# Twelve pairs of the down projection in the 7-product form, with two of the weight sums on GpSimd

## The chip, the core and the metric

The kernel runs on one NeuronCore of a Trainium2 chip. The metric is the device time of one execution in microseconds (us). Five engines work side by side, each through its own instructions in order: TensorE (PE, matmuls; PEld are its weight loads), VectorE (DVE), ScalarE (ACT), GpSimd (POOL) and SyncE (SP, which here only issues loads and stores). An instruction waits for semaphores that other engines raise, and what stands behind it on its engine waits as well.

## The reference

One decoder layer for 256 tokens of width 2048, all in float32: three mixers side by side (pooling, latent attention, attention to a memory), an output projection, and a gated feed-forward part with a short convolution. The change lies in the last part:

```
def conv_glu_ffn(h, w_gate, w_up, conv_w, conv_b, w_down):
    g = h @ w_gate                       # 256 x 5632
    gp = jnp.pad(g, ((0, 0), (CONV_WIDTH - 1, 0), (0, 0)))
    gc = conv_b
    for j in range(CONV_WIDTH):
        gc = gc + conv_w[j] * gp[:, j:j + S]
    return (jax.nn.silu(gc) * (h @ w_up)) @ w_down   # 5632 -> 2048
...
x = x + conv_glu_ffn(rms_norm(x, g_ffn[l]), ...)
```

## The kernel before

**Precision.** Each float32 operand of a large matrix product is split into a rounded high part and a low part, the rest. ACT writes the high part (`wh`, L98), DVE the low part (`wl = raw - wh`, L99), and PE adds three products: high by high, low by high, high by low. A tile of 1024 columns of weights so costs one ACT and one DVE instruction; there are four buffers for `wh` and four for `wl`, and three for raw weights (`wr`), which SP fills with 1 MB loads.

**Gate and up.** The 5632 features are 44 blocks of 128. For each block f, `gemm_pair` computes gate and up (L134), and `glu` adds the halves of the two sums: `halves` copies one half from PSUM on ACT (L784) and adds the other on DVE (L785). For gate this is in the buffer `g`, for up in the buffer `u`, one buffer each. DVE and ACT then make the convolution and the Silu in `gc`, DVE multiplies (L801 or L809), and the result is split as the left operand of the down projection (L158, L159).

**The down projection** takes two blocks at a time, as 22 pairs j, and goes through them twice, once for each half c of the 2048 output columns. A pair is a 2x2 block product: two token halves, two feature blocks, two column quarters of 512.
- A *plain* pair makes 8 block products of 3 matmuls each, 24 matmuls of 128x512, from two weight tiles of 1024 columns.
- A pair in the *7-product form* makes 7 block products, 21 matmuls (the Strassen-Winograd scheme). `glu` prepares its left operand: four sums of 128x128 (L813) and a split of 128x896 (L816, L817), in 7 KB per partition instead of the 4 KB of a plain pair. `seven` makes sums of the weights: `F13` (T1 and T3, one DVE instruction, L880), then T2 = r2 - T1 (L882) and T4 = r3 - T2 (L883), `F24` together. It then splits four tiles: `b11` (512 columns), `b2`, `t13`, `t24` (1024 each).
- `SEVEN` lists the pairs in this form, 11 of 22.

Four PSUM banks hold the sums of one half's own products, four the common products. `common` adds the latter to the residual near the end of a half (L905, L909), `finish` adds the former and stores (L916, L917). The residual comes back from HBM by four GpSimd loads per half (L901). The first half's stores are issued by GpSimd too, in pair 0 of the second half.

**Order.** A scheduler orders each engine's instructions; those marked with `keep` stay in program order. In the down projection all ACT and DVE splits after pair 1 of the first half are kept. The weight tile of every fourth pair goes to a part of `dn` (L850) instead of `wr`. Buffers of `F13` and `F24` are the first four 512-column pieces of `dn`, and swap from one 7-product pair to the next.

**The ring.** GpSimd's own DMAs (`nc.gpsimd.dma_start`) take their descriptors from a ring, whose size per partition is an argument at L1017.

Of the kernel before, what the change touches and what calls it, by code (L numbers as in the profile page):

```python
# [15 lines left out]
ALU = mybir.AluOpType  # L16
# [22 lines left out]
NN = 512  # L39

PAIRS = KF // 2
SEVEN = (1, 2, 4, 5, 7, 9, 11, 13, 15, 17, 19)

VEC = [
    ("g_mix", KD), ("g_ffn", KD), ("g_q_lat", QR // P), ("g_kv_lat", KVR // P),
# [15 lines left out]
def layer(ctx, tc, xT_d, xn_d, memT_d, vec_d, tab_d, w_z_d, w_mqkr_d, w_q_d, w_kv_d, w_mem_d, w_pool_d, w_o_d,  # L61
          w_g_d, w_u_d, w_dn_d, out_d):
    nc = tc.nc
# [8 lines left out]
    def nm(s):  # L72
        uid[0] += 1
        return f"{s}_{uid[0]}"
# [13 lines left out]
    def keep(ins, on=True):  # L88

        return tc.keep_in_program_order(ins) if on else ins  # L90

    def split_w(raw, o, n, cut=HS, kept=False, shift=0):

        hi = stage.tile([P, HS], F32R, tag="wh", name=nm("wh"), bufs=4)
        lo = stage.tile([P, HS + 64], F32R, tag="wl", name=nm("wl"), bufs=4)[:, shift:shift + HS]
        for c in range(0, n, cut):
            e = min(n, c + cut)
            keep(nc.scalar.copy(hi[:, c:e], raw[:, o + c:o + e]), kept)  # L98
            keep(nc.vector.tensor_tensor(lo[:, c:e], raw[:, o + c:o + e], hi[:, c:e].bitcast(F32), op=ALU.subtract),  # L99
                 kept)  # L100
        return hi, lo
# [53 lines left out]
    def split_act(dst, src, scale=None, kept=False):  # L155

        if scale is None:
            nc.scalar.copy(dst[:, 0:T], src)  # L158
            nc.vector.tensor_tensor(dst[:, T:2 * T], src, dst[:, 0:T].bitcast(F32), op=ALU.subtract)  # L159
        else:  # L160
            keep(nc.scalar.activation(dst[:, 0:T], src, AF.Copy, scale=scale), kept)
            keep(nc.vector.scalar_tensor_tensor(dst[:, T:2 * T], src, scale, dst[:, 0:T].bitcast(F32),
                                                op0=ALU.mult, op1=ALU.subtract), kept)
# [4 lines left out]
    def v(name, i=0):  # L168
        o = VOFF[name] + i
        return vec[:, o:o + 1]  # L170
# [610 lines left out]
    def halves(ps, tag):  # L781

        t = fp.tile([P, T], F32, tag=tag, name=nm(tag), bufs=1)
        nc.scalar.copy(t[:], ps[:, 0:T])  # L784
        nc.vector.tensor_tensor(t[:], t[:], ps[:, T:2 * T], op=ALU.add)  # L785
        return t

    def glu(f, psg, psu):
        g = halves(psg, "g")
        nc.vector.tensor_tensor(g[:], g[:], r1[:], op=ALU.mult)  # L790
        gc = fp.tile([P, T], F32, tag="gc", name=nm("gc"), bufs=1)
        nc.scalar.activation(gc[:], g[:], AF.Identity, bias=v("conv_b", f), scale=v("cw2", f))  # L792
        for d, w in ((1, "cw1"), (2, "cw0")):
            nc.vector.scalar_tensor_tensor(gc[:, d:T], g[:, 0:T - d], v(w, f), gc[:, d:T], op0=ALU.mult, op1=ALU.add)  # L794
        nc.scalar.activation(gc[:], gc[:], AF.Silu)
        u = halves(psu, "u")
        j, e = f // 2, f % 2
        if j not in SEVEN:
            if e == 0:
                aT[j] = fp.tile([P, 2, 2 * T], F32R, name=nm("aT"))  # L800
            nc.vector.tensor_tensor(u[:], u[:], gc[:], op=ALU.mult)  # L801
            split_act(aT[j][:, e, :], u[:])
            return
        if e == 0:
            aT[j] = fp.tile([P, 2, 7, P], F32R, name=nm("aS"))
            hold[j] = fp.tile([P, 8, P], F32, tag="s8", name=nm("s8"), bufs=1)
        s = hold[j]
        o = 0 if e else 6
        nc.vector.tensor_tensor(s[:, o:o + 2, :].rearrange("p a t -> p (a t)"), u[:], gc[:], op=ALU.mult)  # L809
        if e:  # L810
            for d, a, op, b in ((2, 7, ALU.add, 1), (3, 2, ALU.subtract, 6), (4, 6, ALU.subtract, 7),
                                (5, 0, ALU.subtract, 3)):
                nc.vector.tensor_tensor(s[:, d, :], s[:, a, :], s[:, b, :], op=op)  # L813
            hi, lo = (aT[j][:, i].rearrange("p a t -> p (a t)") for i in range(2))
            sf = s[:, 0:7, :].rearrange("p a t -> p (a t)")
            nc.scalar.copy(hi, sf)  # L816
            nc.vector.tensor_tensor(lo, sf, hi.bitcast(F32), op=ALU.subtract)  # L817
# [10 lines left out]
    for ps, raw in zip(pss, raws):  # L828
        gemm_t(ps, raw, HS, lambda k: h2[:, k, :], range(8, KD), first=False)
    glu(0, *pss)  # L830
    for f in range(1, KF):
        pss = [ps_main() for _ in range(2)]
        gemm_pair(pss, [load_w(w[f], STG) for w in (w_g_d, w_u_d)], lambda k: h2[:, k, :])
        glu(f, *pss)
# [9 lines left out]
    def load_dn(c, j):  # L844

        cnt[1] += 1
        if cnt[1] % 4:
            return load_w(w_dn_d[c, j], STG)
        raw = dn[:, 4:8].rearrange("p b n -> p (b n)")
        nc.sync.dma_start(raw, w_dn_d[c, j])  # L850
        return raw

    def prod(ps, a, b, first, last):

        nc.tensor.matmul(ps, a[0], b[0], start=first, stop=False)  # L855
        nc.tensor.matmul(ps, a[1], b[0], start=False, stop=False)  # L856
        nc.tensor.matmul(ps, a[0], b[1], start=False, stop=last)  # L857
# [15 lines left out]
    def seven(c, j, own, com, first, last, kept):  # L873
        raw = load_dn(c, j)
        r3 = raw.rearrange("p (b n) -> p b n", n=NN)

        i = cnt[0] % 2
        cnt[0] += 1
        F13, F24 = dn[:, 2 * i:2 * i + 2], dn[:, 2 - 2 * i:4 - 2 * i]
        keep(nc.vector.tensor_tensor(F13, r3[:, 1:3], r3[:, 0:2], op=ALU.subtract), kept)  # L880
        b11 = split_w(raw, 0, NN, kept=kept)
        keep(nc.vector.tensor_tensor(F24[:, 0], r3[:, 2], F13[:, 0], op=ALU.subtract), kept)  # L882
        keep(nc.vector.tensor_tensor(F24[:, 1], r3[:, 3], F24[:, 0], op=ALU.subtract), kept)  # L883
        b2 = split_w(raw, 2 * NN, HS, kept=kept)
        t13 = split_w(F13.rearrange("p b n -> p (b n)"), 0, HS, kept=kept)
        t24 = split_w(F24.rearrange("p b n -> p (b n)"), 0, HS, kept=kept)
        for (b, s), f, ps, own_ in (((b11, 0), 6, com[0], False), ((b2, 0), 5, own[0, 1], True),
                                    ((b2, 1), 0, own[0, 0], True), ((t13, 0), 2, com[1], False),
                                    ((t13, 1), 4, com[3], False), ((t24, 0), 3, com[2], False),
                                    ((t24, 1), 1, own[1, 0], True)):  # L890
            prod(ps, [aT[j][:, i, f, :] for i in range(2)], [w[:, s * NN:(s + 1) * NN] for w in b],
                 first and not own_, last and not own_)
# [29 lines left out]
    for c in range(2):  # L922
        own_ps, com_ps = (ps_main, ps_aux) if c else (ps_aux, ps_main)
        own = {(t, n): own_ps()[:] for t in range(NT) for n in range(2)}
        com = None
        for j in range(PAIRS):
            kept = c > 0 or j > SEVEN[0]
            if j in SEVEN:
                if com is None:
                    com = [com_ps()[:] for _ in range(4)]  # L930
                seven(c, j, own, com, j == SEVEN[0], j == SEVEN[-1], kept)
            else:
                between = None
                if j == 0 and done is not None:
                    between = lambda o=done: finish(0, o, nc.gpsimd)
                elif j >= PAIRS - 2:
                    between = lambda s=j - PAIRS + 3: common(c, com, s)
                plain(c, j, own, j == 0, j == PAIRS - 1, kept, between, j == PAIRS - 1)
            if j == PAIRS - 6:
                common(c, None, 0)  # L940
        done = own
# [85 lines left out]
```

## Time and profile before

| what | value |
|---|---|
| time, median of 3 runs | 1004.43 us (1003.9 to 1004.48) |
| profiled execution: time, span | 1004.47 us, 1002.7 us |
| PE busy | 996.4 us (99%) |
| DVE busy | 767.4 us (77%) |
| ACT busy | 586.6 us (58%) |
| POOL busy | 18.5 us (2%), 39 instructions |
| DMA | 200.17 MB, mean 200 GB/s |

The profile shows one execution. In a *timeline*, a row gives start, duration, engine, line, operation, output<-input, shape and count, and in brackets how long the engine was idle before and what ended that. In a *group* row, the figures behind the bars are busy time and mean ns of one, then idle time before it and what ended most of it. In the view of *busy time by stretch*, each row gives the stretch, its length, then busy time (and count) of PE, PEld, DVE, ACT and POOL, the granted clock of PE, the DMA share and GB/s. Matmuls are pipelined: a row's duration is longer than the distance to the next start.

### The profile page before, as it was taken

The page shows a single profiled execution, that of the slowest core. Times are in us where ns is not written, and L with a number is a line of the kernel's source. Part 1 is how long each engine was busy: PE and PEld are TensorE (multiplying, and loading weights), DVE is VectorE, ACT ScalarE, POOL GpSimd, SP SyncE. Part 2 cuts the span into 40 slices and gives each one's busy share as a digit, 9 for nine tenths or more (in the row PEclk, how much of TensorE's full clock was granted, in tenths as well). Part 3 has the DMA queues.
Part 4 walks back from the last instruction along what each step waited for, and adds up shares of the span by engine and source line. Part 5 has one row for each costly group of instructions (what it writes and reads, how often), then busy time and mean ns, then how long its engine had stood idle before and what let it go on. Part 6 is the DMA issues. An engine that isn't in the chain of part 4 may idle for free.

```text
span 1002.7 us, 14022 instructions
## 1 busy us (share of the span) xinstructions
PE 996.4 (99%) x5342; PEld 859.7 (86%) x5342; DVE 767.4 (77%) x1160; ACT 586.6 (58%) x859; POOL 18.5 (2%) x39
## 2 busy tenths in 40 slices
PE   9999999999999999999999999999999999999998
PEld 8898888888888888888888888888888888888886
DVE  6778689855677776777776767777677998899887
ACT  7678666544566555555555655555565656545562
POOL 1010000000000000000000000000000000010000
PEclk9999999999999999999999999999999999999999
DMA  9867443433664555455555555555556665486651
GB/s 356 294 239 277 151 173 150 157 139 128 229 230 169 186 196 206 171 207 182 197 197 189 203 175 203 190 189 205 190 194 221 221 230 210 169 293 213 220 197 42
DMA packets 31764, 200.17 MB, mean 200 GB/s; under 512 B 3664, under 2 KB 4176, under 8 KB 9808
## 3 DMA queue, kind: packets, MB, share of 16 engines
q1 hardware_dynamic: 28512, 189.04, 52.6%
q0 software_dynamic: 2752, 9.44, 2.7%
q8 instruction: 42, 0.69, 0.3%
q10 hardware_dynamic: 432, 0.79, 0.2%
q14 instruction: 26, 0.21, 0.1%
HBM read 195.06 MB, written 4.19 MB: 199 GB/s over the span
## 4 chain that ended last, share of the span: by engine, by line
PE 96%; DVE 3%; issue 1%; ACT 0%; DVEq 0%; ACTq 0%
PE psm L134 47%; PE psm L117 7%; PE psm L151 5%; PE psm L152 5%; PE psm L153 5%; PE psa L855 3%; PE psa L857 3%; PE psm L857 3%; PE psa L856 3%; PE psm L856 3%; PE psm L855 3%; DVE wl L99 1%; PE psa L679 1%; PE psa L151 1%; PE psa L153 1%
## 5 line engine op out<-in xcount | busy, mean ns | idle before, releaser
L99 DVE TENSOR_TENSOR wl<-wr,wh 128x1024 fp32r<-128x1024 f32 (+2 forms) x338 | 391.4, 1172 | 131.6 <-ACT wh L98 75.2
L98 ACT CAST wh<-wr 128x1024 fp32r<-128x1024 f32 (+2 forms) x338 | 340.4, 1012 | 133.4 <-PE psm L134 55.4
L134 PE MATMUL psm<-h,wh 128*128 128x512 f32 x1376 | 320.1, 390 | 0.0
L134 PEld LDWEIGHTS psm<-h,wh 128*128 128x128 f32 x1376 | 255.1, 188 | 51.3
L134 PEld LDWEIGHTS psm<-h,wl 128*128 128x128 f32 x1376 | 163.8, 188 | 3.3
L134 PE MATMUL psm<-h,wl 128*128 128x256 f32 x1376 | 164.5, 277 | 0.0
L98 ACT CAST wh<-dn 128x1024 fp32r<-128x1024 f32 (+1 forms) x66 | 65.4, 995 | 79.5 <-PE psa L856 31.9
L99 DVE TENSOR_TENSOR wl<-dn,wh 128x1024 fp32r<-128x1024 f32 (+1 forms) x66 | 74.0, 1146 | 16.0 <-ACT wh L98 16.0
L792 ACT ACTIVATE gc<-g,vec 128x256 f32<-128x256 f32 x44 | 26.5, 602 | 93.3 <-DVE g L790 93.3
L794 DVE SCALAR_TENSOR_TENSOR gc<-g,vec,gc 128x255 f32<-128x255 f32 x88 | 42.5, 483 | 33.0 <-ACT gc L792 31.4
L117 PE MATMUL psm<-xg,wh 128*128 128x512 f32 x160 | 39.9, 393 | 0.0
L151 PE MATMUL psm<-wh,cat 128*128 128x512 f32 x96 | 38.2, 398 | 0.0
L153 PE MATMUL psm<-wl,cat 128*128 128x512 f32 x96 | 37.4, 390 | 0.0
L152 PE MATMUL psm<-wh,cat 128*128 128x512 f32 x96 | 37.4, 389 | 0.0
L855 PE MATMUL psa<-wh,aT 128*128 128x512 f32 x88 | 34.3, 389 | 0.0
L856 PE MATMUL psa<-wh,aT 128*128 128x512 f32 x88 | 34.2, 389 | 0.0
L856 PE MATMUL psm<-wh,aT 128*128 128x512 f32 x88 | 34.2, 389 | 0.0
L855 PE MATMUL psm<-wh,aT 128*128 128x512 f32 x88 | 34.2, 389 | 0.0
L857 PE MATMUL psa<-wl,aT 128*128 128x512 f32 x88 | 33.9, 389 | 0.0
L117 PEld LDWEIGHTS psm<-xg,wh 128*128 128x128 f32 x160 | 29.1, 188 | 5.4
L857 PE MATMUL psm<-wl,aT 128*128 128x512 f32 x88 | 33.3, 389 | 0.0
L784 ACT COPY g<-psm 128x256 f32<-128x256 f32 x44 | 16.5, 375 | 27.7 <-PE psm L134 27.7
(234 smaller groups left out, 1420.9 us busy)
## 6 DMA issues: line engine op xcount, KB each, us to landing
wr<-in_w_g SPq DMA_DIRECT2D x44, 1024.0 KB, 4.8
wr<-in_w_u SPq DMA_DIRECT2D x44, 1024.0 KB, 4.8
wr<-in_w_dn SPq DMA_DIRECT2D x33, 1024.0 KB, 4.8
wr<-in_w_o SPq DMA_DIRECT2D x16, 1024.0 KB, 4.8
dn<-in_w_dn SPq DMA_DIRECT2D x11, 1024.0 KB, 4.8
wr<-in_w_z SPq DMA_DIRECT2D x10, 1024.0 KB, 6.8
wr<-in_w_mem SPq DMA_DIRECT2D x6, 1024.0 KB, 8.4
wr<-in_w_mqkr SPq DMA_DIRECT2D x8, 576.0 KB, 5.0
```

The costliest lines, as they stand in the source:

```text
L98: keep(nc.scalar.copy(hi[:, c:e], raw[:, o + c:o + e]), kept)
L99: keep(nc.vector.tensor_tensor(lo[:, c:e], raw[:, o + c:o + e], hi[:, c:e].bitcast(F32), op=ALU.subtract), kept)
L117: keep(nc.tensor.matmul(ps[:, T if low else 0:2 * T], w, act(k)[:, 0:T] if low else act(k), start=first and c + i == 0 and not low, stop=l ...
L134: nc.tensor.matmul(ps[:, T if low else 0:2 * T], parts[k // nk][low][:, i * P:(i + 1) * P], act(k)[:, 0:T] if low else act(k), start=k == ...
L151: keep(nc.tensor.matmul(ps, xh, hi[:, i, o], start=first and i == 0, stop=False), kept)
L152: keep(nc.tensor.matmul(ps, xl, hi[:, i, o], start=False, stop=False), kept)
L153: keep(nc.tensor.matmul(ps, xh, lo[:, i, o], start=False, stop=last and i == nk - 1), kept)
L792: nc.scalar.activation(gc[:], g[:], AF.Identity, bias=v("conv_b", f), scale=v("cw2", f))
L794: nc.vector.scalar_tensor_tensor(gc[:, d:T], g[:, 0:T - d], v(w, f), gc[:, d:T], op0=ALU.mult, op1=ALU.add)
L855: nc.tensor.matmul(ps, a[0], b[0], start=first, stop=False)
L856: nc.tensor.matmul(ps, a[1], b[0], start=False, stop=False)
L857: nc.tensor.matmul(ps, a[0], b[1], start=False, stop=last)
```

## The change

Four lines change. `SEVEN` gets a twelfth pair: pairs 8, 10 and 12 come in and 9 and 11 go out, so that 7 and 8, and 12 and 13, stand side by side. The two weight sums T2 and T4 are made by GpSimd instead of VectorE. Up's half sums use the buffer of gate's (tag `g`), so there is no buffer `u`. The descriptor ring is 1 KB instead of 2 KB. The last two free 2 KB per partition, and the twelfth pair's left operand takes 3 KB more than before.

```diff
-SEVEN = (1, 2, 4, 5, 7, 9, 11, 13, 15, 17, 19)
+SEVEN = (1, 2, 4, 5, 7, 8, 10, 12, 13, 15, 17, 19)
...
-        u = halves(psu, "u")
+        u = halves(psu, "g")
...
-        keep(nc.vector.tensor_tensor(F24[:, 0], r3[:, 2], F13[:, 0], op=ALU.subtract), kept)
-        keep(nc.vector.tensor_tensor(F24[:, 1], r3[:, 3], F24[:, 0], op=ALU.subtract), kept)
+        keep(nc.gpsimd.tensor_tensor(F24[:, 0], r3[:, 2], F13[:, 0], op=ALU.subtract), kept)
+        keep(nc.gpsimd.tensor_tensor(F24[:, 1], r3[:, 3], F24[:, 0], op=ALU.subtract), kept)
...
-    nc = _bacc.Bacc("TRN2", target_bir_lowering=False, num_devices=1, dynamic_dma_scratch_size=2048)
+    nc = _bacc.Bacc("TRN2", target_bir_lowering=False, num_devices=1, dynamic_dma_scratch_size=1024)
```

VectorE's program for pair 2 of the second half and the plain pair behind it, before (numbers behind names are buffers; L880 is F13, the 128x512 split is b11, then T2, T4, b2, t13, t24 and the plain pair's two tiles):

```order
L880 TENSOR_TENSOR dn<-wr_8292 128x1024
L99 TENSOR_TENSOR wl_8296<-wr_8292,wh_8295 128x512
L882 TENSOR_TENSOR dn<-wr_8292,dn 128x512
L883 TENSOR_TENSOR dn<-wr_8292,dn 128x512
L99 TENSOR_TENSOR wl_8302<-wr_8292,wh_8301 128x1024
L99 TENSOR_TENSOR wl_8306<-dn,wh_8305 128x1024
L99 TENSOR_TENSOR wl_8310<-dn,wh_8309 128x1024
L99 TENSOR_TENSOR wl_8337<-wr_8334,wh_8336 128x1024
L99 TENSOR_TENSOR wl_8341<-wr_8334,wh_8340 128x1024
```

and of the change:

```order
L880 TENSOR_TENSOR dn<-wr_8303 128x1024
L99 TENSOR_TENSOR wl_8307<-wr_8303,wh_8306 128x512
L99 TENSOR_TENSOR wl_8313<-wr_8303,wh_8312 128x1024
L99 TENSOR_TENSOR wl_8317<-dn,wh_8316 128x1024
L99 TENSOR_TENSOR wl_8321<-dn,wh_8320 128x1024
L99 TENSOR_TENSOR wl_8348<-wr_8345,wh_8347 128x1024
L99 TENSOR_TENSOR wl_8352<-wr_8345,wh_8351 128x1024
```

L882 and L883 are gone from between b11 and b2; the rest keeps its order.

GpSimd's program from the residual's stores on, before:

```order
L358 DMA s_85_699<-in_xn 128x1024
L743 DMA x1s<-x1n 128x512 x8
L901 DMA dn<-x1s 128x512 x4
L917 DMA out_t<-dn 128x512 x4
L901 DMA dn<-x1s 128x512 x4
L1023 UNCONDITIONAL_BRANCH
```

and of the change, from the first half's stores on to pair 2 of the second half:

```order
L917 DMA out_t<-dn 128x512 x4
L901 DMA dn<-x1s 128x512 x2
L882 TENSOR_TENSOR dn<-dn 128x512
L901 DMA dn<-x1s 128x512
L883 TENSOR_TENSOR dn<-dn 128x512
L901 DMA dn<-x1s 128x512
L882 TENSOR_TENSOR dn<-wr_8303,dn 128x512
L883 TENSOR_TENSOR dn<-wr_8303,dn 128x512
```

T2 and T4 of pair 1 (its weights lie in `dn`) now stand between the four reloads of the residual, behind the four stores. In the change, ACT's high part of t24 waits for GpSimd instead of VectorE. SP's program is the same in both, and PE's has six matmuls fewer in each execution.

## The prediction

> **What bounds the kernel now.** I read the page's engine totals first, then the busy time by stretch, then the timelines of PE and DVE in the down projection.
>
> ```profile
> span 1002.7 us, 14022 instructions
> PE 996.4 (99%) x5342; PEld 859.7 (86%) x5342; DVE 767.4 (77%) x1160; ACT 586.6 (58%) x859; POOL 18.5 (2%) x39
> ...
> 400.00:500.00 100.00, 100.00 (x585) 88.30 (x584) 73.66 (x112) 57.62 (x81) 0.00 (x0) 1.00 0.55 191
> ...
> 800.00:900.00 100.00, 99.62 (x440) 81.88 (x439) 90.78 (x98) 55.85 (x60) 4.32 (x8) 1.00 0.64 224
> ```
>
> PE is busy nearly always, at a granted clock of 1.00. DVE (third pair of numbers in a stretch) has slack in gate and up, 73.66 of 100 us, and little in the down projection, 90.78. Busy shares of PE hide short gaps, because a matmul's 0.39 us overlaps the next; so I count starts.
>
> ```profile
> 771.89 0.39 PE L855 MATMUL psa<-wh,aT 128*128 128x512 f32 x1
> ...
> 849.82 0.39 PE L855 MATMUL psa<-wh,aS 128*128 128x512 f32 x1
> ...
> 858.44 0.39 PE L857 MATMUL psa<-wl,aT 128*128 128x512 f32 x1
> ...
> 893.38 0.39 PE L855 MATMUL psa<-wh,aS 128*128 128x512 f32 x1
> ...
> 897.78 0.50 PE L855 MATMUL psa<-wh,aS 128*128 128x512 f32 x1 [0.38 <-ACT wh L98]
> ...
> 997.62 0.39 PE L857 MATMUL psm<-wl,aT 128*128 128x512 f32 x1
> ```
>
> From 849.82 to 858.44 lie 38 starts: a pitch of 0.2268 us. A plain pair (24 matmuls) takes PE 5.44 us, a pair in the 7-product form (21) 4.76 us. The whole projection is 990 matmuls, 22 pairs of each kind: 989 pitches are 224.3 us, and first to last start is 225.7. So PE loses only some 1.4 us there; the gap at 897.78, which ended when ACT's high part came, is a piece of it.
>
> Now DVE for one 7-product pair and the plain pair behind it:
>
> ```profile
> 893.41 1.23 DVE L880 TENSOR_TENSOR dn<-wr 128x1024 f32<-128x1024 f32 x1
> 894.55 0.69 DVE L99 TENSOR_TENSOR wl<-wr,wh 128x512 fp32r<-128x512 f32 x1
> 895.15 0.68 DVE L882 TENSOR_TENSOR dn<-wr,dn 128x512 f32<-128x512 f32 x1
> 895.87 0.69 DVE L883 TENSOR_TENSOR dn<-wr,dn 128x512 f32<-128x512 f32 x1
> 896.48 1.22 DVE L99 TENSOR_TENSOR wl<-wr,wh 128x1024 fp32r<-128x1024 f32 x1
> 897.62 2.35 DVE L99 TENSOR_TENSOR wl<-dn,wh 128x1024 fp32r<-128x1024 f32 x2
> 899.89 2.35 DVE L99 TENSOR_TENSOR wl<-wr,wh 128x1024 fp32r<-128x1024 f32 x2
> 902.16 1.22 DVE L880 TENSOR_TENSOR dn<-wr 128x1024 f32<-128x1024 f32 x1
> ```
>
> The first form costs DVE 899.89 - 893.41 = 6.48 us, 1.72 more than PE; the plain one 2.27, 3.17 less. Two 7-product pairs and a plain one: 15.23 on DVE, 14.96 on PE. PE sets the pace, and DVE is just behind it.
>
> **The change, part by part.** *The twelfth pair* takes 3 matmuls out of each column half: 6 x 0.2268 = 1.4 us less PE. With all of the 1.4 us of gaps gone as well, the most that can be won is 2.8 us.
>
> *T2 and T4 on POOL* take L882 and L883 from DVE: 896.48 - 895.15 = 1.33 us a pair, which leaves 5.15. What a sum of 128x512 takes on POOL the trace does not show; its nearest rows:
>
> ```profile
> L560 POOL MEMSET qkv<- 128x2048 f32 x1 | 1.8, 1813 | 6.7 <-PE psm L153 6.7
> ...
> masks.py:199 POOL TENSOR_SCALAR_AFFINE_SELECT identf<-identf 128x128 f32<-128x128 f32 x1 | 0.3, 291 | 0.0
> ...
> masks.py:197 POOL MEMSET identf<- 128x128 f32 x1 | 0.2, 205 | 0.3 <-POOLq L1017 0.3
> ...
> L1017 POOL MEMSET const-float32-0.0<- 128x1 f32 x1 | 0.1, 99 | 0.2 <-issue 0.2
> ```
>
> Writing costs (205 - 99)/128 = 0.83 ns an element; reading one operand as well adds (291 - 205)/128 = 0.67. With two operands 512 elements come to 0.10 + 512 x (0.83 + 0.67 + 0.67) = 1.21 us. The bounds: 0.53 (written only, the large memset's slope) and 2.3 (four affine selects, doubled for the second operand). I take 1.21. The Trainium skill's "GPSIMD Engine Reference", section 3.1, has 4497 ns for a two-input add of 2048 elements; a quarter, 1.12, is an estimate from that page, which no run here shows, and would give some 4 us less than my sum.
>
> The price that decides is another: **how long DVE stands still for one POOL sum**. Call it x. The only row of a longer POOL instruction beside DVE work is this:
>
> ```profile
> 50.37 1.81 POOL L560 MEMSET qkv<- 128x2048 f32 x1 [6.66 <-PE psm L153]
> ...
> 50.82 0.76 DVE L99 TENSOR_TENSOR wl<-wr,wh 128x576 fp32r<-128x576 f32 x1 [1.95 <-ACT wh L98]
> ...
> L99 DVE TENSOR_TENSOR wl<-wr,wh 128x576 fp32r<-128x576 f32 x16 | 11.7, 753 | 8.2 <-ACT wh L98 8.2
> ```
>
> DVE's 0.76 us beside the memset is its mean: x = 0. But the memset reads nothing, while each T sum reads two streams from SBUF, and so does every DVE instruction of such a pair. So x lies between 0 and the whole sum, 1.21, or more if waits add up; below 0 is excluded, since DVE's own instructions do not get shorter. I take 1.21, because the one undisturbed row differs in just this point. The Trainium skill says so outright ("SBUF — State Buffer", section "Who interferes with whom"): a DVE instruction with two SBUF inputs contends with a GpSimd instruction that reads SBUF, and the one that comes second waits for the other to end; no run here shows it. By that rule x is the sum's whole time; without it 0, and the time that of the first rival.
>
> With x = 1.21 a 7-product pair costs DVE 5.15 + 2.42 = 7.57 us. DVE keeps its program order here, so it cannot go ahead of a late instruction: behind the low part of T24 stands the next pair's L880, and PE waits for both. Two 7-product pairs and a plain one: 17.41 against 14.96, late by 2.45. One and one: 9.84 against 10.20, early by 0.36. The list now has three groups of the first kind in pairs 1 to 9, one in 12 to 14, and alternates elsewhere. The ends of the halves add:
>
> ```profile
> L909 DVE SCALAR_TENSOR_TENSOR dn<-dn,rc 128x512 f32<-128x512 f32 x8 | 5.5, 743 | 0.0
> L916 DVE SCALAR_TENSOR_TENSOR dn<-psm,rc,dn 128x512 f32<-128x512 f32 x4 | 2.8, 745 | 0.7 <-PE psm L857 0.7
> ...
> L905 DVE TENSOR_TENSOR dn<-dn,psm 128x512 f32<-128x512 f32 x4 | 2.7, 685 | 1.0 <-PE psm L857 0.9
> ```
>
> Four of each, 0.08 us overlapped: 7.9 us, beside two plain pairs that give 6.3 back. DVE's lead at the start:
>
> ```profile
> 778.39 1.23 DVE L99 TENSOR_TENSOR wl<-dn,wh 128x1024 fp32r<-128x1024 f32 x1 [0.60 <-ACT wh L98]
> ...
> 781.18 0.39 PE L857 MATMUL psm<-wl,aS 128*128 128x512 f32 x1
> ```
>
> Pair 1's last low part ends at 779.6 and is used at 781.2: 1.5 us. So the first half loses 3 x 2.45 - 1.5 = 5.9, then 2.45 - 0.36 = 2.1, then at its end 7.9 - 6.3 - 3 x 0.36 = 0.5; the second 7.35 and 2.1. Together **17.9 us**.
>
> *POOL's queue at the start of the second half.* The sums of pair 1 now stand behind the four stores and between the four reloads.
>
> ```profile
> 889.09 1.12 POOL L901 DMA_DIRECT2D dn<-x1s  x2 [2.46 <-DMA out_t<-dn]
> 891.35 0.54 POOL L901 DMA_DIRECT2D dn<-x1s  x1 [1.14 <-DMA out_t<-dn]
> ...
> 890.08 1.05 ACT L98 CAST wh<-dn 128x1024 fp32r<-128x1024 f32 x1 [0.88 <-DVE dn L883]
> ```
>
> T2 runs from 890.2 to 891.4, the third reload to 892.0, T4 to 893.2, ACT's high part to 894.3, where it ended at 891.1 before. PE wants it at 893.38: with the low part behind it some 1.7 us, if DVE is on time. With x = 1.21 DVE is later than that anyway, and I count nothing.
>
> *Up's half sums in gate's buffer.* The order on ACT and DVE stays, so the question is whether the buffer is free in time.
>
> ```profile
> 654.25 0.42 DVE L159 TENSOR_TENSOR aT<-u,aT 128x256 fp32r<-128x256 f32 x1
> ...
> 657.22 0.38 ACT L784 COPY g<-psm 128x256 f32<-128x256 f32 x1 [0.80 <-PE psm L134]
> ...
> L813 DVE TENSOR_TENSOR s<-s 128x128 f32<-128x128 f32 x44 | 12.7, 290 | 1.1
> L817 DVE TENSOR_TENSOR aS<-s,aS 128x896 fp32r<-128x896 f32 x11 | 12.0, 1093 | 11.1 <-ACT aS L816 11.1
> ```
>
> The last reader of u ends at 654.67, the next gate copy starts at 657.22: 2.5 us to spare. One more pair prepared for the 7-product form adds 4 x 0.29 + 1.09 - 2 x 0.42 = 1.4 us of DVE to two feature blocks; DVE's 26 us idle in each 100 of that stage cover it. *The ring*: POOL's waits are the same; if each of 4 stores waited out the one before, the second half would start several us later, and I take nothing.
>
> The sum: 17.9 - 1.4 (matmuls) - 1.4 (gaps, which the new waits contain) = +15.1 on the profiled execution's own 1004.47 us (span 1002.7 and 1.8 around it; the median of the runs is 1004.43): **1019.5 us**. With x = 1.0 the same steps give 1010.6, with x = 1.5, 1032.
>
> **The rivals.**
> *DVE is not held up (not slower).* x = 0, its point being 0.60: up to there two 7-product pairs and a plain one stay under 14.96. Then the chain L880, T2, T4, ACT's high part 1.05 takes 3.5 us after L880, and DVE has 2.9 us of other work: 0.6 us of waiting, 5.8 a pair, still under today's 6.48. PE remains the bound: 1004.5 - 1.4 - 1.4 + 1.7 (start of the second half) = 1003.3. For it: the memset row. Against it: that row reads nothing.
> *The two share by the element.* DVE stands only while POOL reads: 2 x 512 x 0.67 ns = 0.69. The groups are late by 0.4, and with the 1.7 us the time is 1004.4; at 0.85, 1007.
> *POOL gets its turn only when DVE idles.* T2 and T4 then start when DVE runs out of work before T24: 5.15 + 2.42 + 1.05 = 8.6 a pair, 4.5 late per group: 1043.
> *The change does not do what it says*: excluded, PE's program has 6 matmuls fewer in groups of three.
>
> **How the numbers follow.** Held up whole 0.60 (own range 1010 to 1032); shared by element 0.12; not held up 0.18; POOL last 0.10. The range is 1003 to 1033; it leaves out the last case and the lower edge of the third. Within 0.2%, about what a measurement can tell from no change, is 1002.4 to 1006.4: 0.21, from the second and third cases. Faster 0.06, if the gaps go and the second half starts on time. Slower 0.73.
>
> **What would show it.** In the changed profile: the means of L99 and L880 in the down projection (1219 ns now) above 1.4 us, or idle time of DVE beside POOL sums; T2 and T4 near 1.2 us or longer by a wait; PE gaps in pairs 1 to 9 and 12 to 14 of both halves, ended by ACT or DVE, and about 18 us in all; gate and up unchanged. Wrong would be means of 1.22 us beside POOL sums with a dense PE; or sums well off 1.21 us, at 4 us of time for each 0.1.

## The result, and the profile after

| | before | after |
|---|---|---|
| time, median (lowest to highest) | 1004.45 us (1003.9 to 1004.69, 4 runs) | 1022.82 us (1022.51 to 1022.87, 4 runs) |
| ratio after to before, 95% interval | | 1.0183 [1.017, 1.0196] |
| profiled span | 1002.7 us | 1021.1 us |
| PE, DVE, ACT, POOL busy | 996.4, 767.4, 586.6, 18.5 us | 1000.8, 798.8, 587.8, 107.0 us |

The change made the kernel 18.4 us slower; the forecast was 1019.5 us. The changed kernel's page gives the totals of the engines, and its view of busy time by stretch shows where they changed (columns as in the prediction: PE, PEld, DVE, ACT, POOL, granted clock, DMA share, GB/s):

```profile
span 1021.1 us, 14117 instructions
PE 1000.8 (98%) x5336; PEld 858.7 (84%) x5336; DVE 798.8 (78%) x1125; ACT 587.8 (58%) x862; POOL 107.0 (10%) x87
```

```profile
400.00:500.00 100.00, 100.00 (x584) 88.32 (x583) 74.79 (x115) 57.99 (x81) 0.00 (x0) 1.00 0.54 190
800.00:900.00 100.00, 95.23 (x414) 76.75 (x413) 97.03 (x77) 51.15 (x55) 37.37 (x26) 1.00 0.57 197
```

Read the two stretches against those of before. Gate and up are unchanged: PE is full, DVE has 74.79 us where it had 73.66. In the down projection PE fell from 99.62 to 95.23 and DVE rose from 90.78 to 97.03, although DVE issues fewer instructions (77 against 98 in the stretch, 1125 against 1160 in all). An engine with less to do and more busy time must have longer instructions. The groups of the down projection, with shapes kept apart, show which:

```profile
L99 DVE TENSOR_TENSOR wl<-dn,wh 128x1024 fp32r<-128x1024 f32 x63 | 106.4, 1705 | 5.6 <-ACT wh L98 4.9
L99 DVE TENSOR_TENSOR wl<-wr,wh 128x1024 fp32r<-128x1024 f32 x47 | 75.3, 1625 | 0.0
...
L883 POOL TENSOR_TENSOR dn<-wr,dn 128x512 f32<-128x512 f32 x17 | 36.1, 2126 | 1.3
...
L882 POOL TENSOR_TENSOR dn<-wr,dn 128x512 f32<-128x512 f32 x17 | 27.2, 1602 | 80.9 <-issue 53.6 <-ACT wh L98 27.3
L880 DVE TENSOR_TENSOR dn<-wr 128x1024 f32<-128x1024 f32 x17 | 20.8, 1221 | 0.7 <-PE psm L134 0.5
...
L99 DVE TENSOR_TENSOR wl<-wr,wh 128x512 fp32r<-128x512 f32 x17 | 11.6, 685 | 0.3 <-ACT wh L98 0.3
```

The same two groups of splits before:

```profile
L99 DVE TENSOR_TENSOR wl<-dn,wh 128x1024 fp32r<-128x1024 f32 x57 | 67.9, 1219 | 16.0 <-ACT wh L98 16.0
L99 DVE TENSOR_TENSOR wl<-wr,wh 128x1024 fp32r<-128x1024 f32 x51 | 60.7, 1218 | 0.0
```

The 128x1024 splits (L99) take 1705 and 1625 ns on average where they took 1219 and 1218. L880 and the 512-column split have not changed: 1221 and 685 ns. Taken one by one, only what stands right behind b11 in program order, b2 and t13, has grown: they take 2.30 to 2.33 us in 22 of the 24 pairs, while t24 and the plain pairs' splits still take 1.22 or 1.23. One pair on DVE's timeline:

```profile
904.20 1.22 DVE L880 TENSOR_TENSOR dn<-wr 128x1024 f32<-128x1024 f32 x1
905.34 2.91 DVE L99 TENSOR_TENSOR wl<-wr,wh 128x512 fp32r<-128x512 f32 x2
908.18 3.56 DVE L99 TENSOR_TENSOR wl<-dn,wh 128x1024 fp32r<-128x1024 f32 x2
911.65 2.35 DVE L99 TENSOR_TENSOR wl<-wr,wh 128x1024 fp32r<-128x1024 f32 x2
913.92 1.22 DVE L880 TENSOR_TENSOR dn<-wr 128x1024 f32<-128x1024 f32 x1
```

and POOL's timeline beside it:

```profile
905.57 1.60 POOL L882 TENSOR_TENSOR dn<-wr,dn 128x512 f32<-128x512 f32 x1 [3.26 <-issue]
907.25 2.15 POOL L883 TENSOR_TENSOR dn<-wr,dn 128x512 f32<-128x512 f32 x1
```

T2 starts on the record at 905.57, while b11 is under way (from 905.34; its successor starts 0.6 us later where nothing holds it), and ends at 907.17; b2, which should end some 1.1 us after b11, ends at 908.2. T4 starts at 907.25, while b2 is under way, and ends at 909.4; t13 and t24 together take 3.56 us where two splits took 2.35. The two engines take turns: b11, T2, b2, T4, t13. The recorded 1.60 and 2.15 us of the sums hold the wait for the DVE instruction ahead. Where DVE idles, a sum takes 1.31 or 1.29 us (the rows of the second half's start, below). The pair costs DVE 911.65 - 904.20 = 7.45 us. Its own instructions would be 5.15, so one sum holds DVE for (7.45 - 5.15) / 2 = 1.15 us.

What PE waits for in the down projection, in the view of waits (us in total, times, longest):

```profile
PE psa L857 <- DVE wl L99: 7.0, 9, 1.2
PE psm L857 <- DVE wl L99: 5.6, 8, 1.2
PE psa L855 <- ACT wh L98: 1.8, 1, 1.8
```

Counting starts as in the prediction: PE's 984 matmuls run from 771.70 to 1015.96, that is 244.26 us where 983 pitches of 0.2268 are 222.9. The gaps are 21.3 us, against 1.4 before. 21.3 - 1.4 - 1.4 (six matmuls) = 18.5 us, the whole loss. They lie in the second pair of each two neighbouring 7-product pairs, and at the start of the second half in both; in the alternating stretches there is none.

### The profile page after: what moved, and what is told of

Its sections match the earlier page's. It is cut to its first block, busy times and chain, and to the rows that moved or that the text cites. A ratio compares the mean times of both kernels' runs of the same rounds, so it can differ in the third digit from the quotient of the medians.

```text
span 1021.1 us, 14117 instructions
## 1 busy us (share of the span) xinstructions
PE 1000.8 (98%) x5336; PEld 858.7 (84%) x5336; DVE 798.8 (78%) x1125; ACT 587.8 (58%) x862; POOL 107.0 (10%) x87
## 4 chain that ended last, share of the span: by engine, by line
PE 91%; issue 4%; DVE 3%; POOL 1%; DMA 0%; ACT 0%; DVEq 0%; POOLq 0%
PE psm L134 46%; PE psm L117 7%; PE psm L151 5%; PE psm L153 5%; PE psm L152 5%; PE psm L857 3%; DVE wl L99 3%; PE psm L856 3%; PE psm L855 3%; PE psa L857 3%; PE psa L856 2%; PE psa L855 2%; PE psa L679 1%; PE psa L151 1%; PE psa L153 1%
## 5 line engine op out<-in xcount | busy, mean ns | idle before, releaser
L99 DVE TENSOR_TENSOR wl<-wr,wh 128x1024 fp32r<-128x1024 f32 (+2 forms) x338 | 407.8, 1223 | 130.2 <-ACT wh L98 74.5
L98 ACT CAST wh<-dn 128x1024 fp32r<-128x1024 f32 (+1 forms) x70 | 69.8, 1009 | 100.6 <-POOL dn L883 55.1
L99 DVE TENSOR_TENSOR wl<-dn,wh 128x1024 fp32r<-128x1024 f32 (+1 forms) x70 | 110.6, 1603 | 5.6 <-ACT wh L98 4.9
L784 ACT COPY g<-psm 128x256 f32<-128x256 f32 x88 | 32.8, 373 | 45.6 <-PE psm L134 45.0
L901 POOL DMA_DIRECT2D dn<-x1s x8 | 4.4, 552 | 486.3 <-PE psm L134 483.0
L857 PE MATMUL psa<-wl,aS 128*128 128x512 f32 x84 | 34.3, 408 | 7.0 <-DVE wl L99 7.0
L857 PE MATMUL psm<-wl,aS 128*128 128x512 f32 x84 | 33.9, 403 | 5.6 <-DVE wl L99 5.6
L785 DVE TENSOR_TENSOR g<-g,psm 128x256 f32<-128x256 f32 x88 | 36.5, 415 | 0.5 <-ACT g L784 0.5
L883 POOL TENSOR_TENSOR dn<-wr,dn 128x512 f32<-128x512 f32 x17 | 36.1, 2126 | 1.3
L882 POOL TENSOR_TENSOR dn<-wr,dn 128x512 f32<-128x512 f32 x17 | 27.2, 1602 | 80.9 <-issue 53.6
L855 PE MATMUL psa<-wh,aS 128*128 128x512 f32 x84 | 33.1, 394 | 1.8 <-ACT wh L98 1.8
```

## The experiments

All times are beside runs of the kernel before on the same chip (1004.2 to 1004.5 us). Below, a time without a ratio beside it is that of a single execution; one with a ratio is the median of 11. "PE gaps" are the distances between starts beyond the pitch, where that is 0.02 us or more; on this count before has 1.3 us and the changed kernel 20.9.

### Extra POOL work that nobody waits for

Three kernels leave all of DVE's work as it was before and add to each 7-product pair after pair 2 two POOL instructions whose result nothing waits for on the way to PE. All three share up's and gate's buffer and have the 1 KB ring. They differ in what POOL reads: two operands, one, none.

```diff
+        if j > 2:
+            for n in range(2):
+                keep(nc.gpsimd.tensor_tensor(sc[:], r3[:, 2 + n], F13[:, n], op=ALU.subtract), kept)  # side_sums
+                keep(nc.gpsimd.tensor_copy(sc[:], F13[:, n]), kept)                                  # side_copies
+                keep(nc.gpsimd.memset(F24, 0.0), kept)                         # side_memsets, ahead of F13
```

Two sums:

> This kernel is the one before (11 pairs, T2 and T4 on VectorE) with up's half sums in gate's buffer and the 1 KB ring, and with two more subtractions of 128x512 on GpSimd in each 7-product pair from pair 4 on, whose operands lie in SBUF and whose result nobody reads. Theory (VectorE stands still for the whole of a GpSimd sum that reads SBUF): a 7-product pair costs VectorE 6.48 + 2.3 = 8.8 us; the group 4 to 6 is late by 4.9, each of the seven alternating pairs by 0.85, so some 11 us a half: 1025 (1020 to 1030), and the means of VectorE's 1024-column splits rise well above 1219 ns in these pairs. Rival (the loss came from the chain of waits through T4 and ScalarE): nobody waits for these sums, so 1004.5 (1003.5 to 1006).

Measured: 1023.65 us. DVE's groups L886 and L887 are T2 and T4 here (683 and 691 ns before), L884 is the extra sum:

```profile
L99 DVE TENSOR_TENSOR wl<-dn,wh 128x1024 fp32r<-128x1024 f32 x57 | 74.3, 1347 | 0.6 <-ACT wh L98 0.6
...
L884 POOL TENSOR_TENSOR sc<-wr,dn 128x512 f32<-128x512 f32 x20 | 34.9, 1744 | 79.2 <-issue 53.6 <-DVE dn L881 24.8
...
L887 DVE TENSOR_TENSOR dn<-wr,dn 128x512 f32<-128x512 f32 x13 | 18.1, 1394 | 1.0
...
L886 DVE TENSOR_TENSOR dn<-wr,dn 128x512 f32<-128x512 f32 x13 | 15.5, 1190 | 0.0
```

No chain of results connects these sums with DVE, and still DVE's instructions grow by up to 0.7 us in the mean, while DVE idles hardly at all ahead of them (0.0 to 1.0 us in a whole group). DVE's busy time is 802.5 us instead of 767.4, over 36 sums 0.98 us for each. The cost is POOL's reading beside DVE, not a new wait for a result.

Two copies:

> As the run with idle subtractions, but with two GpSimd copies of 128x512 in each pair from 4 on: they read one operand where the subtraction reads two. Theory: a read is enough, and VectorE stands for the copy's length, by estimate from the affine select (1.5 ns an element) 0.87 us each: 8.2 us a pair, group 3.7, alternates 0.3 each, about 1015 (1009 to 1019). Rival (only two-operand sums hold VectorE up, or none): 1004.5.

Measured: 1007.23 us, below the expected range.

```profile
L884 POOL COPY sc<-dn 128x512 f32<-128x512 f32 x36 | 38.1, 1059 | 143.9 <-DVE dn L881 142.8
...
L887 DVE TENSOR_TENSOR dn<-wr,dn 128x512 f32<-128x512 f32 x13 | 11.3, 871 | 1.0
...
L886 DVE TENSOR_TENSOR dn<-wr,dn 128x512 f32<-128x512 f32 x13 | 10.9, 841 | 0.0
```

One operand read holds DVE too, but by (779.1 - 767.4) / 36 = 0.33 us a copy, a third of a sum's. The expectation took too much for it.

Two memsets:

> As the run with idle subtractions, but with two GpSimd memsets of 128x1024 into the buffer of T2 and T4 before VectorE writes it, in each pair from 4 on: about 0.96 us each, writes only. Theory (it is the reading that excludes VectorE): 1004.5 (1003.5 to 1006), and VectorE's means stay at 1.22 us. Rival (any GpSimd work beside VectorE holds it up): 1.9 us a pair, about 1016.

Measured: 1003.87 us.

```profile
L99 DVE TENSOR_TENSOR wl<-dn,wh 128x1024 fp32r<-128x1024 f32 x57 | 67.8, 1219 | 16.1 <-ACT wh L98 16.1
...
L882 POOL MEMSET dn<- 128x1024 f32 x36 | 34.4, 957 | 131.3 <-DVE wl L99 130.3
```

36 memsets, 34.4 us of POOL, move DVE's mean by nothing. The same run prices the shared buffer and the small ring: nothing.

### Which DVE instructions are held

Two extra sums (of a tile minus itself, into a scratch tile) beside the adds of `common`, which read one operand from PSUM and one from SBUF; shared buffer and 1 KB ring as above.

```diff
+            for _ in range(2):
+                keep(nc.gpsimd.tensor_tensor(sc[:], v1, v1, op=ALU.subtract))
             ... # then the four DVE adds of L905
```

> The kernel before with the shared buffer for half sums, the 1 KB ring and two extra GpSimd subtractions of 128x512 out of two SBUF tiles in each pair's step in which VectorE adds products from PSUM to SBUF tiles (their result is read by nothing). Theory: only VectorE instructions that read two SBUF operands are held by GpSimd's reads; the adds out of PSUM read one, so their mean stays near what it was (within 10%), a GpSimd subtraction takes about 1.3 us, and the time stays within 2 us of 1004.4. Rival: any VectorE instruction that touches SBUF is held; then these adds grow by 0.3 to 0.6 us each where a subtraction runs, GpSimd's grow to 1.6 us or more, and the time rises by some 10 us or more.

Measured: 1004.31 us. DVE's and POOL's timeline at the first of the two places (the adds are L908 here):

```profile
870.70 1.22 DVE L99 TENSOR_TENSOR wl<-wr,wh 128x1024 fp32r<-128x1024 f32 x1
872.80 2.73 DVE L908 TENSOR_TENSOR dn<-dn,psm 128x512 f32<-128x512 f32 x4 [0.89 <-PE psm L858]
```

```profile
871.03 2.90 POOL L906 TENSOR_TENSOR sc<-dn 128x512 f32<-128x512 f32 x2 [96.57 <-ACT dn L904]
```

The sums run until 873.93, so the first 1.1 us of the adds lie beside them, and the four take 2.73 us as they did before (687 ns each). So these adds, with one operand in PSUM, were not held. The overlap is short, at two places, and the sums read one tile twice; more than this the run does not show.

### The parts of the change

Only T2 and T4 on POOL, eleven pairs:

> The kernel before with only T2 and T4 moved to GpSimd: 11 pairs, own buffer u, 2 KB ring. Theory: a 7-product pair costs VectorE 7.45 us; the groups 1 to 3 and 4 to 6 lose 2.3 each, in the second half's first group 3.4 more by GpSimd's queue, alternating pairs nothing: 12.5 less the 1.3 of gaps that go into it, 1015.7 (1012 to 1018). Rival (the twelfth pair, the shared buffer or the ring made the loss): 1004.5.

Measured: 1015.34 us, PE gaps 12.9 us. Only the twelfth pair, T2 and T4 left on DVE (with the list, shared buffer and ring of the change):

```diff
-        keep(nc.gpsimd.tensor_tensor(F24[:, 0], r3[:, 2], F13[:, 0], op=ALU.subtract), kept)
-        keep(nc.gpsimd.tensor_tensor(F24[:, 1], r3[:, 3], F24[:, 0], op=ALU.subtract), kept)
+        keep(nc.vector.tensor_tensor(F24[:, 0], r3[:, 2], F13[:, 0], op=ALU.subtract), kept)
+        keep(nc.vector.tensor_tensor(F24[:, 1], r3[:, 3], F24[:, 0], op=ALU.subtract), kept)
```

> The changed kernel with T2 and T4 back on VectorE: 12 pairs, shared buffer, 1 KB ring. Theory (only the move of the sums costs): 6 matmuls less are 1.4 us, two neighbouring pairs and a plain one are late by 0.27 on VectorE, four such groups a half, so 1003 to 1004.5, at or a little under the kernel before. Rival (VectorE cannot feed a twelfth pair): about 1008.

Measured: 1003.92 us, ratio to before 0.9996 [0.9987, 1.0006]: not to be told from no change. PE gaps are 2.1 us, so of the 1.4 us that six matmuls less give, 0.8 went into four more groups of neighbours.

So the parts do not add up: -0.4 and +11.2 alone, +18.4 together. The list of twelve has four groups of neighbours in a half where the list of eleven has two, and a group loses time only where a pair costs DVE more than about 6.35 us (half of 14.96 - 2.27).

The twelve pairs spread differently, DVE making the sums:

```diff
-SEVEN = (1, 2, 4, 5, 7, 8, 10, 12, 13, 15, 17, 19)
+SEVEN = (1, 2, 4, 6, 8, 9, 11, 13, 14, 16, 18, 19)
```

> As the last, with the 12 pairs spread as 1, 2, 4, 6, 8, 9, 11, 13, 14, 16, 18, 19, so that no two groups of neighbours follow each other. Theory: the 1.45 us that an alternating pair gives back comes between the groups; gaps of PE under 1 us in all, 1002.5 to 1003.3. Rival (the place does not matter): the same as the last within 0.3 us.

Measured: 1006.05 us, ratio 1.0019 [1.001, 1.0028]: a miss. PE gaps are 2.9 us, no fewer. The profiled executions of this run and the one before it took 1007.13 and 1003.74 us; 2.3 of these 3.4 us lie behind the last matmul, where the last four stores take longer to land. The views of DMAs from 985 us on give the median from issue to landing, in the run before this one

```profile
out_t<-dn SPq DMA_DIRECT2D x4, 256.0 KB, 2.6
```

and in this one

```profile
out_t<-dn SPq DMA_DIRECT2D x4, 256.0 KB, 4.3
```

Why these stores land later was not found out.

### Half as many sums on POOL

If each sum costs 1.15 us, T4 alone on POOL should halve the loss.

```diff
-        keep(nc.gpsimd.tensor_tensor(F24[:, 0], r3[:, 2], F13[:, 0], op=ALU.subtract), kept)
+        keep(nc.vector.tensor_tensor(F24[:, 0], r3[:, 2], F13[:, 0], op=ALU.subtract), kept)
```

> The changed kernel with T2 back on VectorE and only T4 on GpSimd. Theory: one GpSimd sum holds VectorE up by 1.15 us and saves it 0.66, so a 7-product pair costs 7.0 us; groups of neighbours lose 1.2 each, the alternating pairs give 0.9 back, and the second half's start waits 2 to 3 us for GpSimd's queue: 1011 (1007 to 1014). Rival (the loss is a fixed cost of handing work to GpSimd at all, not of each sum): about 1020.

Measured: 1025.12 us, slower than with both sums on POOL: a miss. POOL's timeline in a pair that follows a plain one, and DVE's:

```profile
791.08 3.19 POOL L883 TENSOR_TENSOR dn<-wr,dn 128x512 f32<-128x512 f32 x1 [7.18 <-DVE dn L882]
```

```profile
788.42 1.22 DVE L880 TENSOR_TENSOR dn<-wr 128x1024 f32<-128x1024 f32 x1
...
790.76 1.22 DVE L99 TENSOR_TENSOR wl<-wr,wh 128x1024 fp32r<-128x1024 f32 x1
791.90 1.22 DVE L99 TENSOR_TENSOR wl<-dn,wh 128x1024 fp32r<-128x1024 f32 x1
795.38 1.22 DVE L99 TENSOR_TENSOR wl<-dn,wh 128x1024 fp32r<-128x1024 f32 x1 [2.26 <-ACT wh L98]
796.64 1.22 DVE L880 TENSOR_TENSOR dn<-wr 128x1024 f32<-128x1024 f32 x1
```

No DVE instruction is longer here: 1.22 us each. It is POOL that stands. T4 is recorded from 791.08, while b2 is under way, but t13 goes ahead of it at 791.90, and T4 ends at 794.27, 1.2 us after t13. By then DVE has nothing left but t24, whose high part waits for T4; it idles 2.26 us. The pair costs 796.64 - 788.42 = 8.2 us, more than with both sums on POOL. This is the prediction's third rival, POOL getting its turn only when DVE idles; the change itself shows it nowhere in these pairs, this kernel in 14 of its 24 sums (3.18 or 3.19 us).

To see what the turn hangs on, T2 was put ahead of b11 on DVE, so that T4 is asked for during b11:

```diff
         keep(nc.vector.tensor_tensor(F13, r3[:, 1:3], r3[:, 0:2], op=ALU.subtract), kept)
+        keep(nc.vector.tensor_tensor(F24[:, 0], r3[:, 2], F13[:, 0], op=ALU.subtract), kept)
         b11 = split_w(raw, 0, NN, kept=kept)
-        keep(nc.gpsimd.tensor_tensor(F24[:, 0], r3[:, 2], F13[:, 0], op=ALU.subtract), kept)
         keep(nc.gpsimd.tensor_tensor(F24[:, 1], r3[:, 3], F24[:, 0], op=ALU.subtract), kept)
```

> The changed kernel with T2 on VectorE, placed ahead of the difference b11, and T4 alone on GpSimd; in the run with T4 alone (1025 us) T2 stood behind b11, so that T4 was asked for when the split t13 was next on VectorE, and was passed over there. Theory: whether a GpSimd sum goes in or is passed over hangs on what VectorE has in hand when the sum is asked for; asked for during b11, T4 goes in behind b11 and ahead of b2, VectorE loses about 1.15 us a pair instead of the whole stand of ScalarE, a pair costs it about 7.0 us, and the run takes about 1011 us (1007 to 1015). Rival: behind a plain pair GpSimd's first sum is always passed over, wherever it is asked for; then T4 again takes some 3.2 us in those pairs and the run about 1025 us (1020 to 1028).

Measured: 1017.02 us, between the two. The mechanism is the theory's: no T4 is passed over any more (20 of 24 take 1.49 to 1.53 us, the longest 2.29).

```profile
788.97 1.21 DVE L880 TENSOR_TENSOR dn<-wr 128x1024 f32<-128x1024 f32 x1
...
796.17 1.23 DVE L880 TENSOR_TENSOR dn<-wr 128x1024 f32<-128x1024 f32 x1
...
803.26 2.35 DVE L99 TENSOR_TENSOR wl<-wr,wh 128x1024 fp32r<-128x1024 f32 x2
```

Two pairs cost DVE 7.20 and 7.09 us, where some 7.0 was expected. The time expected from that was too low by its own figures: with 7.15 a pair, a group is late by 2 x 7.15 + 2.27 - 14.96 = 1.6, and the measured gaps, 1.2 to 2.2 in each of seven groups and 3.9 at the start of the second half, make 14.7 us in all.

### POOL's queue at the start of the second half

The first group of the second half loses 5.7 us in the changed kernel, the like of it elsewhere 2.2 to 2.3. Here the four reloads of the second half are issued much later, so that pair 1's sums stand behind the stores alone:

```diff
-                    nc.gpsimd.dma_start(dn[:, 12 + 2 * t + n, :], x1s[:, t, o:o + NN])
+                    keep(nc.gpsimd.dma_start(dn[:, 12 + 2 * t + n, :], x1s[:, t, o:o + NN]), c > 0)
```

> The changed kernel with the second half's four residual reloads kept in program order, behind the sums of pair 16, so that T2 and T4 of pair 1 no longer stand among them. Theory: the first group of the second half loses 2.3 us as the others do, in place of 5.7: 1019.4 (1018.5 to 1020.5). Rival (VectorE is late there anyway, as the prediction had it, so the queue costs nothing): 1022.8.

Measured: 1021.66 us, in between, and the group loses 4.9 us. First POOL in the changed kernel, then in this one:

```profile
898.18 0.54 POOL L901 DMA_DIRECT2D dn<-x1s  x1 [1.20 <-DMA out_t<-dn]
898.73 1.31 POOL L882 TENSOR_TENSOR dn<-dn 128x512 f32<-128x512 f32 x1
899.96 0.57 POOL L901 DMA_DIRECT2D dn<-x1s  x1
900.54 1.29 POOL L883 TENSOR_TENSOR dn<-dn 128x512 f32<-128x512 f32 x1
```

```profile
895.41 3.88 POOL L882 TENSOR_TENSOR dn<-dn 128x512 f32<-128x512 f32 x1 [1.46 <-issue]
899.37 1.29 POOL L883 TENSOR_TENSOR dn<-dn 128x512 f32<-128x512 f32 x1
```

T2 is asked for 3.3 us earlier, at 895.41, and ends only 0.75 us earlier (of which 0.42 is DVE's earlier start of this pair), because DVE's splits pass it over. DVE's timeline there:

```profile
895.19 2.96 DVE L99 TENSOR_TENSOR wl<-dn,wh 128x512 fp32r<-128x512 f32 x3
901.76 1.23 DVE L99 TENSOR_TENSOR wl<-dn,wh 128x1024 fp32r<-128x1024 f32 x1 [3.62 <-ACT wh L98]
```

The three splits run without a break to 898.15 and T2 ends 1.1 us behind. Taking the queue away gave 0.8 us at this place; the second reason, POOL's turn beside DVE, took its place.

The smaller ring is not the reason for the long group: the kernel with eleven pairs and the 2 KB ring loses 6.3 us in its own. Nor does PE's clock explain it, though in the changed kernel it falls there for 3.4 us; the view of busy time by stretch has:

```profile
904.10:907.40 3.30, 3.18 (x8) 2.50 (x9) 3.27 (x4) 1.32 (x2) 1.75 (x2) 0.50 0.79 302
```

At the granted clock of 0.50 matmuls start 0.43 us apart, and this is counted in the group's 5.7 us. With late reloads the clock stays at 1.00 in the whole projection, and still the group loses 4.9. The 0.8 us between them is what DVE gains: from the start of pair 1's L880 to the start of t24's low part are 8.47 us in the changed kernel and 7.71 with late reloads. PE is waiting for DVE, so the slow matmuls mostly take the place of a later wait.

## Why the prediction was right, and where it was not

**What bounds the kernel, and the groups of pairs.** Right. PE's waits are ended by L99 on DVE (one by ACT) and lie in the groups of two neighbours; alternating stretches have none, as 9.84 against 10.20 said.

**x, how long DVE stands for one sum.** Taken as the sum's whole time, 1.21 us; measured 1.15, with an unhindered sum of 1.29 to 1.31. The sum was estimated 0.1 us too short and DVE stands for less than all of it, so two errors nearly cancel. The pair cost 7.57 us in the forecast and 7.45 to 7.59 (921.51 - 913.92 in the next group) on the chip. The rule quoted from the Trainium skill ("SBUF — State Buffer", section "Who interferes with whom") agrees here: sums that read hold DVE by 0.98 to 1.15 us, memsets by nothing (1219 ns), and adds with an operand in PSUM by nothing (687 ns). For copies, which read one operand, it holds only in part: 0.33 us of 1.06. Its other half, that issue order decides who stands, does not cover these runs: with T4 alone on POOL, T4 was recorded 0.82 us ahead of t13 and ran behind it. Of the signs named, L99's means and longer sums came; L880, named beside L99, kept its 1221 ns, because no sum runs beside it.

**The groups' loss.** A group was to be late by 2.45, and 2.1 in 12 to 14. With the measured 7.45 us a pair the first figure is 2.2, and the first half's gaps are 2.2, 2.3, 2.3 and 1.8. DVE's lead of 1.5 us was to soften the first and did not show; the 0.5 us at the half's end did not come either. First half: 8.7 against 8.5 forecast, by errors that cancel.

**The start of the second half** is the step that was wrong: "With x = 1.21 DVE is later than that anyway, and I count nothing." DVE was not later. It had finished t13 by 898.56 and idled; its row, and ACT's ahead of it:

```profile
902.94 1.22 DVE L99 TENSOR_TENSOR wl<-dn,wh 128x1024 fp32r<-128x1024 f32 x1 [4.38 <-ACT wh L98]
```

```profile
901.86 1.04 ACT L98 CAST wh<-dn 128x1024 fp32r<-128x1024 f32 x1 [5.01 <-POOL dn L883]
```

POOL was the late one, because T2 and T4 stood behind stores and reloads, and PE waited 1.8 us for ACT there. Because POOL's sums ran while DVE idled, they held nothing up, but the idle time was longer than the standing would have been. The group lost 5.7 us where the forecast has 2.45. These 3.3 us are nearly the whole difference between the 17.9 us of the forecast and the 21.3 measured, and between 1019.5 and 1022.8, but only because the rest cancels: the first half lost 0.2 more than forecast, the second half's other groups 0.5 less, and 0.4 lies in steps too small to count as gaps. The prediction's price for the queue, 1.7 us if DVE is on time, added in full would have made 4.2 of the 5.7. How the excess splits between the queue and the turn stays open, since taking away the first brought in the second.

**How near the number came** is in part luck. With x at its measured 1.15, the prediction's steps give some 1017 us: an x a little too large stood in for a part of what was left out at the start of the second half.

**The other edits.** Nothing for buffer, ring and the twelfth pair's preparation: right, by the runs at 1003.87 and 1003.92 us. The 1.4 us for six matmuls is right too.

**The rivals.** "DVE is not held up" and "shared by the element" fall with the pair's 7.45 us and with the run whose sums nobody waits for. "POOL gets its turn only when DVE idles" is wrong for the change's pairs but real in 14 of 24 sums with T4 alone and in one with late reloads. What decides the turn is not settled. With a sum asked for 0.2 to 0.3 us into b11 it went in ahead of b2 in the change and with the early T2, but behind b2 and t13 with late reloads. With T4 alone, a sum asked for 0.3 us into b2 went behind t13 in pairs that follow a plain one, but ahead of it in a second neighbour (816.74, with b2 from 816.43). So the moment of asking alone does not decide it.

## What to carry to other kernels

Work moved from a nearly full VectorE to GpSimd was no relief here, where both read SBUF: it took 0.67 us of VectorE away per sum and cost 1.15 in standing, and the loss shows as longer instructions on VectorE, not as a wait. Price such a move per stretch, against the slack of that stretch, and look at what is queued on GpSimd at the place where the moved work now stands. An edit that is harmless alone, as the twelfth pair, can cost much beside another that takes away the slack it needs.

## What had not been expected of the hardware

- A GpSimd sum can be passed over by VectorE instructions that start after it: by one split in 14 of 24 sums with T4 alone (3.19 us instead of 1.3), by two splits in a row with late reloads (3.88 us).
- A GpSimd copy, which reads one operand, holds VectorE by 0.33 us, not by its whole length (1.06 us in the mean).
- Fewer sums on GpSimd can be slower than more: 1025.1 us with one a pair, 1022.8 with two.
- The granted clock of TensorE was 0.50 for 3.4 us after the waits at the second half's start, in the change and in three other kernels (eleven pairs, T4 alone, early T2). The length of the wait alone does not decide it: it came after a gap of 1.2 us with the early T2 and not after one of 2.8 us with two extra sums.
